# Three decoder-like blocks on one core: rotation by SBUF transfers, a later scaling, matmuls of a bank by kind

## The chip, the cores and the metric

The kernel runs on one core of a Trainium2 chip. The metric is device time in microseconds (us) from start to end of one execution; three executions of the kernel before gave 1177.98, 1178.29 and 1181.79 us, median 1178.29.

## The reference

A sequence of 256 rows of width 1024 in fp32 passes through one block of a first kind and two layers of a second kind. What touches the change is this:

```python
# first block, its end
x = x + jax.nn.sigmoid(x @ w_ple_gate[i]) * (p[i] @ w_ple[i])
return rms_norm(x, final_g)

# second block, per layer
h = rmsnorm(x, g_mix[l])
q_r, k_r, v_r, g_r, q_s, k_s, v_s, gate_a, gate_b = jnp.split(h @ w_in[l], splits, axis=-1)
q_r = rotary(q_r.reshape(B, S, RET_HEADS, RET_QK_DIM), pos)
k_r = rotary(k_r.reshape(B, S, RET_HEADS, RET_QK_DIM), pos) * (RET_QK_DIM ** -0.5)
...
x = x + merged @ w_out[l]
h = rmsnorm(x, g_mlp[l])
up = jnp.square(jax.nn.relu(h @ w_up[l]))
x = x + up @ w_down[l]

def rotary(t, pos):
    ...
    t1, t2 = t[..., :half], t[..., half:]
    return jnp.concatenate([t1 * cos - t2 * sin, t1 * sin + t2 * cos], axis=-1)
```

## The kernel before, in words

Activations stand transposed: 128 features on the partitions, the 256 rows of the sequence along the free axis, so that a tensor of width 1024 is 8 tiles of 128x256. All weights come as a stream of 189 chunks of 1 MB (128 x 2048 fp32). A chunk is fetched by SyncE (SP) into one of three `raw` buffers (`fetch`), then split into a rounded high part `wh` (ScalarE, line 286) and a remainder `wl` (VectorE, line 287), in two halves each (`split`). Activations are split in the same way (`hilo`, lines 127 and 128): a `Pair` holds high and low part of a tile beside each other, 512 columns in all. A product is then high x high, high x low and low x high, all on TensorE.

`mm_t` (line 289) multiplies a chunk of two 128-column blocks: for each block one PSUM bank `acc` (five of them), and for each of the 8 contraction tiles two matmuls. The first (line 295, called **h** here) has `wh` as the weights and streams 512 columns, the high and the low part of the activation at once, into the whole bank. The second (line 297, **l**) has `wl` as weights and streams the 256 columns of the high part into the first half of the bank. They alternate: h, l, h, l, 16 in a bank. `chunk_t` builds such a chunk; 136 of the 189 chunks are of this kind. `fold` (lines 313 and 314) then adds the two halves of the bank, ScalarE copying one and VectorE adding the other. `mm_n` (line 336) and `mm_2` (lines 131 to 133 by `mm3`) are two other forms: `mm_n` runs matmuls of 512 columns by kind, four of a kind in a row, and `mm_2` runs matmuls of 256 columns.

The loop at the end of `tile_blocks` (line 1007) issues per chunk: the split of chunk i+2, the fetch of chunk i+5, the matmuls and evictions of chunk i, and then one step of each waiting generator in `threads` (attention heads, `first_out` and others). The order written so is a starting point: the framework's scheduler reorders the instructions of each engine by a simulated timeline, within the data dependencies. Each engine and each DMA queue then runs its list strictly in order.

The rotation stands in `rot_evac` (lines 793 to 806), for 8 tiles per layer: after the fold, two VectorE products of 64 partitions each multiply the tile by sine and at the same time write the upper half of the partitions to the lower and the reverse (line 801); GpSimd multiplies by cosine (line 802) and adds (line 803); then `hilo`. The tables `n.cr` and `n.sr` (cosine and sine times the norm's factor) are made by `rotary_scales` on GpSimd once the norm's factor is there.

`first_out` (line 678) makes the first block's output, which is needed as residual: it computes the block's own norm factor and scales the 8 tiles of `X` on VectorE (line 687), one chunk after it is added to `threads`. `X` is next read when `w_out` of layer 0 is added to it, some 40 chunks on.

Of the kernel before, what the change touches and what calls it, by code (L numbers as in the profile page):

```python
# [21 lines left out]
S = 256  # L22
# [19 lines left out]
def _tables():  # L42
    f = np.float32
    c = np.zeros((P, C_ALL), f)
    i = np.arange(P)
    c[:, C_ID:C_ID + P] = np.eye(P)
    c[:, C_MQ:C_MQ + P] = np.where(i[None, :] > i[:, None], NEG, 0.0)
    c[:, C_MS:C_MS + P] = np.where(i[:, None] >= i[None, :], NEG, 0.0)
    c[:, C_TRI:C_TRI + P] = np.where(i[:, None] >= i[None, :], -1.0, 0.0)
    inv = (f(500000.0) ** (-np.arange(0, 16, 2, dtype=f) / f(16))).astype(f)  # L50
    ang = (np.arange(S, dtype=f)[:, None] * inv[None, :]).astype(f)
    co, si = np.cos(ang.astype(np.float64)).astype(f), np.sin(ang.astype(np.float64)).astype(f)
    for h in range(2):
        t = slice(h * P, (h + 1) * P)
        b = C_ROPE + 16 * h
        c[:, b:b + 8] = co[t]
        c[:, b + 8:b + 16] = co[t]
        b = C_ROPE + 32 + 16 * h
        c[:, b:b + 8] = -si[t]
        c[:, b + 8:b + 16] = si[t]  # L60
    inv = (f(10000.0) ** (-np.arange(64, dtype=f) / f(64))).astype(f)
    ang = (np.arange(S, dtype=f)[None, :] * inv[:, None]).astype(np.float64)
    c[:64, C_ROT:C_ROT + S] = np.cos(ang)
    c[64:, C_ROT:C_ROT + S] = np.cos(ang)
    c[:64, C_ROT + S:C_ROT + 2 * S] = np.sin(ang)
    c[64:, C_ROT + S:C_ROT + 2 * S] = -np.sin(ang)
    lg = np.log1p(-(2.0 ** (-5.0 - np.arange(4))))
    for h in range(4):
        b = C_DEC + 384 * h
        for off, q, k in ((0, 0, 0), (128, 128, 0), (256, 128, 128)):  # L70
            d = (q + i)[None, :] - (k + i)[:, None]
            c[:, b + off:b + off + P] = np.where(d >= 0, np.exp(lg[h] * np.maximum(d, 0)), 0.0) * 128 ** -0.5
    return c
# [3 lines left out]
def tile_blocks(ctx: ExitStack, tc: tile.TileContext, a: dict, out: bass.AP):  # L77
# [180 lines left out]
    class Chunk:  # L258
# [2 lines left out]


        def __init__(self, parts, banks, shape=(KT, S)):
            self.parts, self.banks, self.shape = parts, banks, shape

    def wcols(w, c, k0=0, kt=KT, n=S):
        return w, k0 * P, kt, c * n
# [20 lines left out]

    def mm_t(ch, ks, xs, j0, evac, n=2):

        for j in range(n):
            ps, w = acc(), slice((j0 + j) * P, (j0 + j + 1) * P)
            for i, (k, x) in enumerate(zip(ks, xs)):
                last = i == len(ks) - 1
                T.matmul(ps, lhsT=ch.wh[:, k, w], rhs=x.rearrange("p c t -> p (c t)"), start=i == 0, stop=last,  # L295
                         skip_group_check=True)
                T.matmul(ps[:, 0:S], lhsT=ch.wl[:, k, w], rhs=x[:, 0], start=False, stop=last, skip_group_check=True)  # L297
            run_pre()
            evac(ps, j)

# [9 lines left out]
    def fold(ps, out=None):  # L310

        t = tl([S], "f", bufs=NF) if out is None else out
        A.activation(t, ps[:, S:2 * S], AF.Copy)  # L313
        V.tensor_add(t, t, ps[:, 0:S])  # L314
        return t
# [27 lines left out]
            with tc.high_priority():  # L343
                pre.pop(0)()

    def chunk_t(w, c, x, evac, k0=0):
        def go(ch):
            mm_t(ch, range(KT), [x().t[:, k] for k in range(KT)], 0, lambda ps, j: evac(ps, 2 * c + j))
        chunks.append(Chunk([wcols(w, c, k0)], go))

    def chunk_2(w, c, x, evac, k0=0):
        def go(ch):
# [312 lines left out]
        hilo(st.n.x.h[:, k], st.n.x.l[:, k], X[:, k])  # L665

    for c in range(4):
        chunk_t(("w_out", 0), c, m_, out1_evac)

    def rotary_scales():  # L670
        n = st.n
# [6 lines left out]
    def first_out():  # L678

        n = st.n  # L680
        yield
        r = tl([W], "nv2")
        rsqrt(r, n.v1)
        yield
        r = r[:, 0:S]
        for k in range(KT):
            V.scalar_tensor_tensor(X[:, k], X[:, k], g_fin[:, k:k + 1], r, ALU.mult, ALU.mult)
            if k % 2:
                yield
# [87 lines left out]
    def layer(l):  # L777
# [15 lines left out]
        def rot_evac(w_):  # L793
            def f(ps, k):
                k -= 4 * w_
                if w_ == 0:
                    first(k)
                n = st.n
                t1, t2 = fold(ps), tl([S], "sig", bufs=4)
                for i, o in ((slice(64, 128), slice(0, 64)), (slice(0, 64), slice(64, 128))):  # L800
                    V.tensor_mul(t2[o], t1[i], n.sr[i])  # L801
                G.tensor_mul(t1, t1, n.cr)
                G.tensor_add(t1, t1, t2)
                d = sl(k // 2, w_)
                hilo(d[0][:, k % 2], d[1][:, k % 2], t1)
            return f

        for u in range(2):
            chunk_t(w, u, x_, rot_evac(0))
            chunk_t(w, 2 + u, x_, rot_evac(1))  # L810

            def ev(ps, h, u=u):
# [95 lines left out]
                yield  # L908

        for c in range(4):  # L910
            chunk_t(("w_out_2", l), c, m_, res_evac(g_mlp[l], mlp_in))

        ups = {}

# [10 lines left out]

        def up(g):
            for c in range(4):
                chunk_t(("w_up_2", l), 4 * g + c, x_, up_evac(g))

        def fin_add(c):  # L930
            def f(ps, h):
# [152 lines left out]
```

## Time and profile before

| what | value |
|---|---|
| median of 3 runs | 1178.29 us |
| the profiled execution | 1178.23 us |
| its span, first to last instruction | 1176.4 us |
| TensorE (PE) busy | 1161.2 us, 99% |
| weight loads of TensorE (PEld) busy | 1011.3 us, 86% |
| VectorE (DVE) busy | 886.9 us, 75% |
| ScalarE (ACT) busy | 706.7 us, 60% |
| GpSimd (POOL) busy | 230.4 us, 20% |
| mean granted TensorE clock | 0.996 |
| DMA | 204.47 MB, mean 174 GB/s |

The span leaves out 1.8 us around the instructions. A matmul's row shows when it starts and how long it takes until its end; the next begins before that end, so the price of a matmul in a stream is the distance of two starts, not its duration.

### The profile page before, as it was taken

What the parts mean: (1) busy time and instruction counts of PE and PEld (TensorE: products, weight loads), DVE (VectorE), ACT (ScalarE), POOL (GpSimd) and SP (SyncE); (2) the same over time, 40 slices, a digit from 0 to 9 for tenths busy, and PEclk for the clock granted to TensorE, in tenths of its full rate; (3) what the DMA queues carried; (4) which work ended last, traced back from release to release, by engine and by line L of the source; (5) the groups of instructions that cost most, each with busy time, mean ns of one, the idle gap of its engine ahead of it and who ended that gap; (6) DMA issues with size and microseconds to landing.
All of it is one profiled execution on the core that took longest, in us unless ns stands there. A gap on an engine that the chain in (4) does not pass through costs nothing.

```text
span 1176.4 us, 17442 instructions
## 1 busy us (share of the span) xinstructions
PE 1161.2 (99%) x6642; PEld 1011.3 (86%) x6642; DVE 886.9 (75%) x1449; ACT 706.7 (60%) x1275; POOL 230.4 (20%) x242
## 2 busy tenths in 40 slices
PE   8999999999999999999999999999999999999997
PEld 6888889997888888888888888888888888888887
DVE  6776768878989676568977777997776667867664
ACT  6657556566457776546745546556867565856452
POOL 1023104124462122202000002653112222000001
PEclk9999999999999999999999999999999999999999
DMA  8443434545335444545555555445444555555540
GB/s 309 180 143 144 146 114 160 202 180 203 144 143 179 148 163 155 190 169 185 209 191 203 180 185 217 162 161 182 159 145 157 190 191 192 184 182 199 192 179 36
DMA packets 29603, 204.47 MB, mean 174 GB/s; under 512 B 3408, under 2 KB 3664, under 8 KB 5584
## 3 DMA queue, kind: packets, MB, share of 16 engines
q1 hardware_dynamic: 29376, 203.34, 48.0%
q8 instruction: 52, 0.85, 0.3%
q14 instruction: 31, 0.25, 0.1%
q10 hardware_dynamic: 144, 0.03, 0.0%
HBM read 202.31 MB, written 1.05 MB: 173 GB/s over the span
## 4 chain that ended last, share of the span: by engine, by line
PE 93%; DVE 5%; issue 1%; ACT 0%; DMA 0%; POOL 0%; POOLq 0%; DVEq 0%; ACTq 0%
PE acc L295 41%; PE acc L297 21%; PE acc L336 19%; PE aux L131 2%; PE aux L133 2%; PE aux L132 1%; PE acc L131 1%; PE acc L132 1%; PE acc L133 1%; DVE wl L287 1%; DVE sig L801 1%; PE aux L458 1%; PE aux L764 1%; PE acc L324 1%; DMA X<-in_xt_dram 0%
## 5 line engine op out<-in xcount | busy, mean ns | idle before, releaser
L287 DVE TENSOR_TENSOR wl<-raw,wh 128x1024 fp32r<-128x1024 f32 (+1 forms) x380 | 463.2, 1253 | 154.4 <-ACT wh L286 152.2
L295 PE MATMUL acc<-X,wh 128*128 128x512 f32 x1472 | 524.7, 398 | 2.5 <-DVE vl L387 1.8
L286 ACT ACTIVATE wh<-raw 128x1024 fp32r<-128x1024 f32 (+1 forms) x380 | 380.7, 1047 | 200.2 <-PE acc L295 131.8
L297 PE MATMUL acc<-X,wl 128*128 128x256 f32 x1472 | 412.6, 281 | 0.0
L295 PEld LDWEIGHTS acc<-X,wh 128*128 128x128 f32 x1472 | 276.6, 188 | 64.5 <-DVE vl L387 2.1
L297 PEld LDWEIGHTS acc<-X,wl 128*128 128x128 f32 x1472 | 278.5, 189 | 2.3
L336 PE MATMUL acc<-wh,X 128*128 128x512 f32 x432 | 112.2, 392 | 0.0
L313 ACT ACTIVATE f<-acc 128x256 f32<-128x256 f32 x216 | 78.7, 372 | 42.2 <-PE acc L297 42.0
L314 DVE TENSOR_TENSOR f<-f,acc 128x256 f32<-128x256 f32 x216 | 86.4, 413 | 22.1 <-ACT f L313 21.3
L336 PEld LDWEIGHTS acc<-wh,X 128*128 128x128 f32 x432 | 79.7, 188 | 15.9
L295 PE MATMUL acc<-A,wh 128*128 128x512 f32 x256 | 90.2, 396 | 0.0
L295 PE MATMUL acc<-B,wh 128*128 128x512 f32 x256 | 90.1, 396 | 0.0
L207 POOL TENSOR_TENSOR sq<-sq,f 128x256 f32<-128x256 f32 x30 | 31.5, 1050 | 268.2 <-ACT f L205 267.6
L589 POOL TENSOR_TENSOR sig<-f,nr 128x256 f32<-128x256 f32 x48 | 42.5, 893 | 148.5 <-DVE f L314 148.4
L297 PE MATMUL acc<-B,wl 128*128 128x256 f32 x256 | 71.4, 279 | 0.0
L297 PE MATMUL acc<-A,wl 128*128 128x256 f32 x256 | 71.3, 279 | 0.0
L295 PE MATMUL acc<-M,wh 128*128 128x512 f32 x192 | 67.1, 397 | 0.0
L658 DVE TENSOR_TENSOR X<-X,acc 128x256 f32<-128x256 f32 x112 | 45.3, 416 | 24.8 <-PE acc L297 23.7
L336 PE MATMUL acc<-wl,X 128*128 128x512 f32 x216 | 59.5, 393 | 0.0
L295 PEld LDWEIGHTS acc<-B,wh 128*128 128x128 f32 x256 | 48.1, 188 | 11.6
L295 PEld LDWEIGHTS acc<-A,wh 128*128 128x128 f32 x256 | 48.1, 188 | 11.3
L297 PE MATMUL acc<-M,wl 128*128 128x256 f32 x192 | 52.7, 280 | 0.0
(224 smaller groups left out, 1744.6 us busy)
## 6 DMA issues: line engine op xcount, KB each, us to landing
raw<-in_wstream_dram SPq DMA_DIRECT2D x187, 1024.0 KB, 4.8
raw<-in_wstream_dram SPq DMA_DIRECT2D x4, 512.0 KB, 7.7
B<-in_tables_dram SPq DMA_DIRECT2D x2, 768.0 KB, 6.8
X<-in_xt_dram SPq DMA_DIRECT2D x2, 512.0 KB, 6.3
out_dram<-M SPq DMA_DIRECT2D x4, 256.0 KB, 2.2
M<-in_g_final_dram SPq DMA_DIRECT2D x1, 512.0 KB, 3.7
cst<-in_tables_dram SPq DMA_DIRECT2D x1, 352.0 KB, 10.0
B<-in_pt_dram SPq DMA_DIRECT2D x1, 256.0 KB, 2.7
```

Source lines behind the costliest of these rows:

```text
L131: T.matmul(o, lhsT=lh, rhs=rh, start=start, stop=False, skip_group_check=True)
L133: T.matmul(o, lhsT=ll, rhs=rh, start=False, stop=stop, skip_group_check=True)
L207: (V if k == KT - 1 else G).tensor_add(sq, sq, t)
L286: A.activation(ch.wh[:, k], ch.raw[:, k], AF.Copy)
L287: V.tensor_sub(ch.wl[:, k], ch.raw[:, k], f32(ch.wh[:, k]))
L295: T.matmul(ps, lhsT=ch.wh[:, k, w], rhs=x.rearrange("p c t -> p (c t)"), start=i == 0, stop=last, skip_group_check=True)
L297: T.matmul(ps[:, 0:S], lhsT=ch.wl[:, k, w], rhs=x[:, 0], start=False, stop=last, skip_group_check=True)
L313: A.activation(t, ps[:, S:2 * S], AF.Copy)
L314: V.tensor_add(t, t, ps[:, 0:S])
L336: T.matmul(p[:, 0:w], lhsT=xs[:, k, t], rhs=ws[:, i, o], start=n == 0 and k == 0, stop=n == 2 and k == KT - 1, skip_group_check=True)
L589: G.tensor_mul(store[(c, i)][0][:, k % 2], fold(ps), st.n.rb)
L658: V.tensor_add(X[:, k], X[:, k], ps[:, o:o + S])
```

## The change

Four edits:

- In `mm_t` the 16 matmuls of a bank are issued by kind, first the 8 h and then the 8 l, unless the chunk is marked `fresh`. Marked are the first chunk behind a norm or a merge: of `w_out`, of the rotated queries, of `w_out_2` and of `w_up_2`, 7 chunks in all.
- In `rot_evac` two transfers from SBUF to SBUF on SP's queue write the halves of the folded tile, exchanged, into the second half of a `sig` buffer; GpSimd writes the product with cosine into the first half; VectorE multiplies the exchanged tile by sine in one instruction of 128 partitions; GpSimd adds.
- The sign of the sine table is turned over, since it is now applied behind the exchange.
- `first_out` waits for twenty steps instead of one.

```diff
     def mm_t(ch, ks, xs, j0, evac, n=2):
         for j in range(n):
             ps, w = acc(), slice((j0 + j) * P, (j0 + j + 1) * P)
-            for i, (k, x) in enumerate(zip(ks, xs)):
-                last = i == len(ks) - 1
-                T.matmul(ps, lhsT=ch.wh[:, k, w], rhs=x.rearrange("p c t -> p (c t)"), start=i == 0, stop=last,
-                         skip_group_check=True)
-                T.matmul(ps[:, 0:S], lhsT=ch.wl[:, k, w], rhs=x[:, 0], start=False, stop=last, skip_group_check=True)
+            kinds = [[(i, n) for i in range(len(ks)) for n in range(2)]] if ch.fresh else \
+                [[(i, n) for i in range(len(ks))] for n in range(2)]
+            for i, n_ in sum(kinds, []):
+                k, x = ks[i], xs[i]
+                if n_ == 0:
+                    T.matmul(ps, lhsT=ch.wh[:, k, w], rhs=x.rearrange("p c t -> p (c t)"), start=i == 0, stop=False,
+                             skip_group_check=True)
+                else:
+                    T.matmul(ps[:, 0:S], lhsT=ch.wl[:, k, w], rhs=x[:, 0], start=False, stop=i == len(ks) - 1,
+                             skip_group_check=True)
             run_pre()
             evac(ps, j)
...
     def first_out():
         n = st.n
-        yield
+        for _ in range(20):
+            yield
         r = tl([W], "nv2")
         rsqrt(r, n.v1)
...
-                t1, t2 = fold(ps), tl([S], "sig", bufs=4)
+                t, s2 = fold(ps), tl([2, S], "sig", bufs=4)
+                t1, t2 = s2[:, 0], s2[:, 1]
                 for i, o in ((slice(64, 128), slice(0, 64)), (slice(0, 64), slice(64, 128))):
-                    V.tensor_mul(t2[o], t1[i], n.sr[i])
-                G.tensor_mul(t1, t1, n.cr)
+                    load(t2[o], t[i])
+                G.tensor_mul(t1, t, n.cr)
+                V.tensor_mul(t2, t2, n.sr)
                 G.tensor_add(t1, t1, t2)
```

How the built order moves is shown at three places. The line numbers of the changed kernel are 7 to 9 higher behind `mm_t`: h is line 300, l is 303, the fold's sum 321, the values' low part 395, the sine product 813.

TensorE, one bank of a gate chunk of layer 0 (`acc` is the bank, `wh` and `wl` the chunk's two parts, `X` the normed activation). Before, the beginning of the bank's 16 rows, of which 16 more follow for the second bank:

```order
L295 MATMUL acc_3423<-X_384_2489,wh_3319 128x512
L297 MATMUL acc_3423<-X_384_2489,wl_3320 128x256
L295 MATMUL acc_3423<-X_384_2489,wh_3319 128x512
L297 MATMUL acc_3423<-X_384_2489,wl_3320 128x256
L295 MATMUL acc_3423<-X_384_2489,wh_3319 128x512
L297 MATMUL acc_3423<-X_384_2489,wl_3320 128x256
```

Of the change, both banks of the same chunk and those of the next:

```order
L300 MATMUL acc_3392<-X_384_2489,wh_3312 128x512 x8
L303 MATMUL acc_3392<-X_384_2489,wl_3313 128x256 x8
L300 MATMUL acc_3416<-X_384_2489,wh_3312 128x512 x8
L303 MATMUL acc_3416<-X_384_2489,wl_3313 128x256 x8
```

The kinds stand apart. In the whole built order an h is directly followed by an l 365 times, where it was 2,100 times.

VectorE, the first four rotated tiles of layer 0 (`f` the folded tiles, `sig` the products with sine, `sr` the sine table, `nr` the norm's factor, `vl` the low part of the retention's values, whose bank it frees). Before:

```order
L233 SCALAR_TENSOR_TENSOR nr_2776<-nt_2792,nr_2776 128x260
L287 TENSOR_TENSOR wl_2993<-raw_2853,wh_2992 128x1024 x2
L801 TENSOR_TENSOR sig_2813<-f_2810,sr_2800 64x256 x2
L801 TENSOR_TENSOR sig_2840<-f_2837,sr_2800 64x256 x2
L801 TENSOR_TENSOR sig_2875<-f_2872,sr_2800 64x256 x2
L801 TENSOR_TENSOR sig_2902<-f_2899,sr_2800 64x256 x2
L387 SCALAR_TENSOR_TENSOR vl_2973<-acc_2924,nr_2776,vh_2972 128x512
```

Of the change:

```order
L321 TENSOR_TENSOR f_2902<-f_2902,acc_2885 128x256
L287 TENSOR_TENSOR wl_2948<-raw_2745,wh_2947 128x1024 x2
L231 TENSOR_TENSOR nt_2792<-nr_2776,nv_426_2778 128x260
L232 SCALAR_TENSOR_TENSOR nt_2792<-nt_2792,nr_2776 128x260
L233 SCALAR_TENSOR_TENSOR nr_2776<-nt_2792,nr_2776 128x260
L287 TENSOR_TENSOR wl_2986<-raw_2855,wh_2985 128x1024
L813 TENSOR_TENSOR sig_2813<-sig_2813,sr_2800 128x256
L813 TENSOR_TENSOR sig_2841<-sig_2841,sr_2800 128x256
L813 TENSOR_TENSOR sig_2877<-sig_2877,sr_2800 128x256
L813 TENSOR_TENSOR sig_2905<-sig_2905,sr_2800 128x256
L395 SCALAR_TENSOR_TENSOR vl_2968<-acc_2921,nr_2776,vh_2967 128x512
```

Four products stand where eight stood, one half of a split has moved behind `vl`, and between the last fold (`f_2902`) and the product that needs its exchange (`sig_2905`) stand three halves of splits, three rows of the norm and three products.

SP's queue at the same place (`raw` are the weight chunks, `B` a table). Before:

```order
L124 DMA B_437_2808<-in_tables_dram 128x1536
L124 DMA raw_2853<-in_wstream_dram 128x2048
L124 DMA raw_2922<-in_wstream_dram 128x2048
L124 DMA raw_2958<-in_wstream_dram 128x2048
L124 DMA raw_2998<-in_wstream_dram 128x2048
```

Of the change:

```order
L124 DMA B_437_2808<-in_tables_dram 128x1536
L124 DMA sig_2813<-f_2810 64x256 x2
L124 DMA raw_2855<-in_wstream_dram 128x2048
L124 DMA sig_2841<-f_2838 64x256 x2
L124 DMA sig_2877<-f_2874 64x256 x2
L124 DMA raw_2919<-in_wstream_dram 128x2048
L124 DMA sig_2905<-f_2902 64x256 x2
L124 DMA raw_2953<-in_wstream_dram 128x2048
```

The exchanges, two per tile and 32 in all, stand among the fetches in the same queue, each behind its fold; the fetches behind them wait in the queue with them.

## Rows read from the trace of the kernel before

**Rows 1.** The page: the chain that ended last, shares of the span by engine.
```profile
PE 93%; DVE 5%; issue 1%; ACT 0%; DMA 0%; POOL 0%; POOLq 0%; DVEq 0%; ACTq 0%
```

**Rows 2.** Waits of PE: engine, line, waited for, total us, times, longest.
```profile
PE acc L295 <- DVE vl L387: 1.8, 1, 1.8
PE aux L133 <- DVE pl L128: 1.5, 2, 1.1
PE acc L295 <- DVE f L314: 0.7, 1, 0.7
```

**Rows 3.** Windows, the whole span, line 297 alone: PE, PEld, clock, DMA.
```profile
0.00:1176.00 1176.00, 608.10 (x2176) 411.03 (x2176) 1.00 0.48 174
```

**Rows 4.** Timeline of PE: start, us, engine, line, tiles; two stretches that alternate.
```profile
452.32 0.40 PE L295 MATMUL acc<-A,wh 128*128 128x512 f32 x1
...
518.39 0.40 PE L295 MATMUL acc<-M,wh 128*128 128x512 f32 x1
...
550.94 0.40 PE L295 MATMUL acc<-X,wh 128*128 128x512 f32 x1
...
719.08 0.39 PE L295 MATMUL acc<-X,wh 128*128 128x512 f32 x1
```

**Rows 5.** Timeline of PE: 512 columns behind 512 columns (line 336, by kind).
```profile
1126.82 1.07 PE L336 MATMUL acc<-wl,A 128*128 128x512 f32 x4
...
1130.45 0.39 PE L336 MATMUL acc<-wh,A 128*128 128x512 f32 x1
```

**Rows 6.** Timeline of PE: 256 columns behind 256 columns (lines 131 to 133).
```profile
235.94 0.28 PE L131 MATMUL acc<-A,wh 128*128 128x256 f32 x1
...
240.74 0.28 PE L132 MATMUL acc<-A,wh 128*128 128x256 f32 x1
```

**Rows 7.** Timeline of PE: four pairs in which kinds stand together by chance.
```profile
524.39 0.62 PE L295 MATMUL acc<-M,wh 128*128 128x512 f32 x2
...
525.80 0.40 PE L295 MATMUL acc<-M,wh 128*128 128x512 f32 x1
```

**Rows 8.** Timeline of PE around its longest wait [idle before, releaser].
```profile
290.89 0.28 PE L297 MATMUL acc<-X,wl 128*128 128x256 f32 x1
292.97 0.61 PE L295 MATMUL acc<-X,wh 128*128 128x512 f32 x1 [1.80 <-DVE vl L387]
...
296.72 0.39 PE L295 MATMUL acc<-X,wh 128*128 128x512 f32 x1
```

**Rows 9.** Timeline of DVE in the same place.
```profile
286.77 5.36 DVE L801 TENSOR_TENSOR sig<-f,sr 64x256 f32<-64x256 f32 x8
292.17 1.41 DVE L387 SCALAR_TENSOR_TENSOR vl<-acc,nr,vh 128x512 fp32r<-128x512 f32 x2
```

**Rows 10.** Lines of DVE, 282 to 346 us: busy us, mean ns | idle before.
```profile
L287 DVE TENSOR_TENSOR wl<-raw,wh 128x1024 fp32r<-128x1024 f32 x18 | 24.7, 1403 | 0.8 <-ACT wh L286 0.7
L801 DVE TENSOR_TENSOR sig<-f,sr 64x256 f32<-64x256 f32 x16 | 10.9, 680 | 0.4
L314 DVE TENSOR_TENSOR f<-f,acc 128x256 f32<-128x256 f32 x10 | 3.9, 407 | 1.4 <-ACT f L313 1.4
...
L687 DVE SCALAR_TENSOR_TENSOR X<-X,gc,nv 128x256 f32<-128x256 f32 x8 | 3.3, 473 | 0.0
```

**Rows 11.** Windows: stretch, PE, PEld, DVE, ACT, POOL busy, granted clock, DMA, GB/s.
```profile
282.00:302.00 20.00, 18.20 (x95) 15.51 (x94) 19.01 (x26) 12.41 (x20) 15.36 (x15) 0.91 0.48 181
390.00:420.00 30.00, 30.00 (x170) 26.20 (x170) 20.48 (x33) 21.83 (x43) 3.91 (x5) 1.00 0.47 169
```

**Rows 12.** Timeline of POOL: the sine table.
```profile
283.90 1.76 POOL L675 TENSOR_TENSOR sr<-cst,nr 128x256 f32<-128x256 f32 x1
```

**Rows 13.** Line 124, all transfers of SP: time from issue to landing.
```profile
DMA to landing us min/median/max: 2.1/4.8/10.8
```

**Rows 14.** Timeline of PE: one h and the l behind it in the slower rhythm.
```profile
222.87 0.40 PE L295 MATMUL acc<-M,wh 128*128 128x512 f32 x1
223.11 0.28 PE L297 MATMUL acc<-M,wl 128*128 128x256 f32 x1
```

More of the change, by code (lines that the diff above doesn't have):

```diff
@@ L64, in _tables @@
     c[64:, C_ROT:C_ROT + S] = np.cos(ang)
-    c[:64, C_ROT + S:C_ROT + 2 * S] = np.sin(ang)
-    c[64:, C_ROT + S:C_ROT + 2 * S] = -np.sin(ang)
+    c[:64, C_ROT + S:C_ROT + 2 * S] = -np.sin(ang)
+    c[64:, C_ROT + S:C_ROT + 2 * S] = np.sin(ang)
     lg = np.log1p(-(2.0 ** (-5.0 - np.arange(4))))
@@ L263, in __init__ @@
         def __init__(self, parts, banks, shape=(KT, S)):
-            self.parts, self.banks, self.shape = parts, banks, shape
+            self.parts, self.banks, self.shape, self.fresh = parts, banks, shape, False
     def wcols(w, c, k0=0, kt=KT, n=S):
@@ L344, in run_pre, with chunk_t @@
                 pre.pop(0)()
-    def chunk_t(w, c, x, evac, k0=0):
+    def chunk_t(w, c, x, evac, k0=0, fresh=False):
         def go(ch):
@@ L349, in chunk_t @@
         chunks.append(Chunk([wcols(w, c, k0)], go))
+        chunks[-1].fresh = fresh
     def chunk_2(w, c, x, evac, k0=0):
@@ L667, in tile_blocks @@
     for c in range(4):
-        chunk_t(("w_out", 0), c, m_, out1_evac)
+        chunk_t(("w_out", 0), c, m_, out1_evac, fresh=c == 0)
     def rotary_scales():
@@ L808, in layer @@
         for u in range(2):
-            chunk_t(w, u, x_, rot_evac(0))
+            chunk_t(w, u, x_, rot_evac(0), fresh=u == 0)
             chunk_t(w, 2 + u, x_, rot_evac(1))
@@ L910, in layer @@
         for c in range(4):
-            chunk_t(("w_out_2", l), c, m_, res_evac(g_mlp[l], mlp_in))
+            chunk_t(("w_out_2", l), c, m_, res_evac(g_mlp[l], mlp_in), fresh=c == 0)
         ups = {}
@@ L927, in up @@
             for c in range(4):
-                chunk_t(("w_up_2", l), 4 * g + c, x_, up_evac(g))
+                chunk_t(("w_up_2", l), 4 * g + c, x_, up_evac(g), fresh=g == 0 and c == 0)
         def fin_add(c):
```

## The prediction

> **What bounds the kernel now.** I read the page first. TensorE makes 93% of the chain that ended last [rows 1], and the table above has it busy for 99% of the span: the time is what PE needs for its list, plus the moments in which it waits. So a change can shorten the run in two ways: a lower price per matmul, or fewer waits of PE. Then the waits of PE: behind the start-up only a few are left, and the four that count all name VectorE as the releaser, 4.0 us together [rows 2]. Then the timeline, for the price of a matmul, which is the distance from one start to the next.
>
> The alternating matmuls run in one of two rhythms. From 452.32 to 518.39 us 187 pairs of h and l follow one another, 353.3 ns a pair; from 550.94 to 719.08 us 485 pairs, 346.7 ns a pair [rows 4]. The reader is to see that the two stretches do the same work at full clock. I counted all stretches of over twenty pairs with nothing between: 1,708 pairs, of which 1,170 are within 0.001 us of the slow rhythm and 538 of the fast one; the mean is 350.7 ns. There are 2,176 pairs in all [rows 3]. What puts a stretch into one rhythm or the other the trace does not say.
>
> The same sizes by kind are in the trace too, in the other two forms. 512 columns behind 512 columns: 16 matmuls from 1126.82 to 1130.45 us, 226.9 ns each [rows 5]. 256 behind 256: 40 matmuls from 235.94 to 240.74 us, 120.0 ns each [rows 6]. Together 346.9 ns, which is the fast rhythm.
>
> **The change part by part.**
>
> *Matmuls by kind.* No matmul and no weight load is added or taken away. In the built order an h directly in front of an l stands 365 times where it stood 2,100 times, so 1,735 pairs leave the alternation. At the mean of 350.7 and a by-kind price of 346.7 (the fast rhythm; rows 5 and 6 agree with it within their rounding) each gives 4.0 ns back: 1,735 x 4.0 = **6.9 us**. The bounds: at most all 2,176 pairs, 8.7 us; at least nothing, since at a place where the scheduler had put kinds together by chance four pairs took 1.41 us, 352.5 ns each [rows 7], the slow rhythm. Below nothing: by kind could settle at the slow rhythm throughout, 1,735 x (353.3 - 350.7) = 4.5 us lost, or worse (rival C). I take 6.9, because rows 5 and 6 are long runs and rows 7 is four pairs that begin and end in alternation. A bank's last high-part matmul now comes half a bank earlier in need of the second half of `wh`; splits are made two chunks ahead, some 11 us (32 pairs), which hides half a microsecond; without that cover PE would wait up to 0.5 us a bank for ScalarE. `wl` is needed later than before.
>
> *VectorE's rotation.* In layer 0 eight tiles cost sixteen products, 10.9 us between 282 and 346 us, mean 680 ns [rows 10]. Eight products of 128 partitions take their place: 407 ns each if nothing disturbs them (the sum of the fold, same shape [rows 10]), up to 680 ns if GpSimd's products beside them slow them as the present ones are; 3.3 to 5.4 us. VectorE gets 5.5 to 7.6 us back there.
>
> *The later scaling.* Eight rows of line 687, 3.3 us [rows 10], and the norm factor's three small ones leave the same stretch, where VectorE is busy 19.01 of 20 us at its start [rows 11]. They come back some twenty chunks on, about 400 us, where VectorE is busy 20.48 of 30 us [rows 11]: they cost nothing there; without that cover they would cost their 3.3 us. ACT's two functions go with them, and its table loads are 13 in both orders.
>
> *What that does to PE.* Its longest wait begins behind the matmul at 290.89 us: the next bank is free only when the values' low part has been read from it, and that stands behind the eight half products of 286.77 us [rows 8, 9]. PE goes on at 292.97 us, 1.97 us late by starts. And then the granted clock is lower: the window from 282 to 302 us shows 0.91 of full speed [rows 11], and six pairs from 292.97 to 296.72 us take 3.75 us where they take 2.10 at 0.350 each [rows 8]: the lower of the two levels, 1.2 GHz, for most of these microseconds behind an idle of two, worth 1.65 us. In the changed order the four products may begin when the sine table is there, 285.66 us [rows 12]; at 407 ns [rows 10] to 670 ns each (5.36/8 [rows 9]) they end by 288.4, and the first half of the values 0.7 us on, at 289.1, before 290.9. So the wait and the clock's fall go. The other waits stand behind the same backlog: VectorE is ahead by over 5 us then, and they are at most 1.1 us each [rows 2]. Sum of what can go: 4.0 us of waits, 0.7 for the overlap that each of the four loses besides, 0.17 in the longest (1.97 by starts against 1.80), 1.65 of clock: 6.4. I take **5.6 us** and leave 0.8 to waits that only shift; bounds 6.4 and 0.
>
> *The transfers.* 32 of 64 KB each are added. The trace has none from SBUF to SBUF; the nearest rows are SP's transfers, 2.1 us at the least, 4.8 in the middle, 10.8 at most from issue to landing [rows 13]. I take 2.2 to 4.8, since the smallest large ones are four times this size. Covers: between the fourth tile's fold and its product VectorE has three halves of splits (1.4 each [rows 10]) and three products (0.41), 5.4 us without the norm's small rows; in the second group of four one half of a split and eight other instructions of at least 0.41, 4.7 us. Up to that a landing costs nothing. The Trainium skill, "DMA: Bandwidth & Descriptors", section "Anatomy of one DMA", puts a fixed 2.0 us and the bytes at 436 GB/s on a transfer from GpSimd's queue, 2.15 us here as an estimate; no run so far shows one from SBUF to SBUF. On SP's queue each stands in front of a fetch and may hold it until a fold is there, a chunk at most (16 pairs, 5.6 us); a fetch is issued three chunks (17 us) ahead of its split and lands in 4.8, so 12 us are spare. I cost it at nothing; if that cover were short, it would be `wh` that is late next.
>
> GpSimd has as many instructions as before, and its product no longer waits for VectorE's reading. Evictions keep their number.
>
> **Sum**, against the profiled execution of 1178.23 us, which is the median of the three runs (1178.29): 1178.2 - 6.9 - 5.6 = **1165.7 us**.
>
> **The rivals.**
>
> *Order is indifferent (A).* The pair costs what it costs, as the four pairs of rows 7 say, and only VectorE's relief counts: 1178.2 - 5.6 = 1172.6. Against it stand the long runs of rows 5 and 6. The Trainium skill, "TensorE: Matmul & The Clock Gate", section "Back-to-back issue gap", speaks for it: its gap, N/2.4 + 2.5 ns warm, depends on the columns alone, 215.8 + 109.2 = 325 ns a pair in either order. By it the term would be 0 and the time 1172.6. The trace disagrees with the figure (346.7 to 353.3) and shows two prices for one sum of columns [rows 4]. Chance 0.17.
>
> *VectorE's relief does not arrive (B).* The products wait for landings as long as they used to compute, so PE's waits stay: 1178.2 - 6.9 = 1171.3. For it: 4.8 us in the middle is near the covers of 4.7 and 5.4, and a fetch of 1 MB may be in flight in front of the exchange. Against it: the size, and the smallest rows at 2.1. If every landing took the worst row's 10.8 us, VectorE would stand 5.4 us in the first group and 6.1 in the second, 11.5 a layer, against some 10 it gets back in layer 0 and 6.5 in layer 1, where no scaling is moved: PE would lose 6.5 us more, 1177.8, which I leave outside the range. Chance 0.12.
>
> *A rhythm of its own (C), the side of slower.* In a run by kind every h would cost what an h costs in the slow rhythm at its worst, 240 ns [rows 14], and every l behind an l 120 [rows 6]: 360 ns a pair in place of 350.7. Over 1,735 pairs that is 16.1 us: 1178.2 + 16.1 - 5.6 = 1188.7. The result is slower from about 356 ns a pair on, where the loss passes 5.6 + 3.5 us. For it: that two rhythms exist shows that a stream can lock to more than one step. Against it: rows 5 hold the same size at 226.9 over a long run, and rows 6 the same operands. Chance 0.04.
>
> *Neither part does anything (D):* kinds indifferent and the waits kept, 1178.2. Chance 0.04.
>
> **How the numbers follow.** Forecast 0.63, A 0.17, B 0.12, C 0.04, D 0.04. The likeliest is 1165.7; its own range, with 6.9 between 4 and 8.7 and 5.6 between 4 and 6.4, is 1163.1 to 1170.2. A and B lie above it, at 1171.3 and 1172.6, and with half of the other's term lost reach 1174.5; below that only an eviction that starts earlier, the first half of a bank being complete 0.96 us before its end, could give more. Range **1162 to 1174.5**. What a measurement of this kernel can tell from no change is about 0.3%, 3.5 us: faster means under 1174.8. Nearly all of the forecast, A and B lie there, so faster 0.88, same 0.07 (D and the edge of A and B), slower 0.05 (C and the edge of D).
>
> **What would show it.** By kind: in any gate or MLP chunk 512-column starts 227 ns apart, then 256-column starts 120 ns apart, 2.78 us a bank; 2.81 to 2.83 says A. VectorE: no wait of PE on line 395 near 291 us and granted clock 1.00 from 282 to 302; products of line 813 of 0.4 to 0.7 us without idle in front of them. An idle of VectorE that names a transfer in front of line 813 says B. Eight rows of line 696 near 400 us with PE without idle there. An h behind an h at 236 ns or more says C. Wrong in size it would be if the two rhythms were there by kind as well, or if PE's waits came back with another name, ScalarE's or SP's.

## The result and the profile after

The changed kernel takes 1169.14 us, median of 4 runs (1168.73 to 1170.5), against 1178.55 before, median of 4 (1177.98 to 1181.79). The ratio is 0.9915, with a 95% interval of 0.9899 to 0.993: faster by 9.4 us, where 12.5 were forecast. The time lies in the range given, 3.4 us above the number. The profiled execution took 1168.73 us, its span 1167.0.

Line numbers have moved: h is now line 300 (295 before), l line 303 (297), the fold 320 and 321 (313, 314), the values' low part 395 (387), the scaling 696 (687), the untransposed matmul 343 (336), and the rotation's products 812 and 813.

The page of the changed kernel, its line of PE and the chain by engine [rows 1]:

```profile
PE 1155.9 (99%) x6642; PEld 1013.0 (87%) x6642; DVE 876.3 (75%) x1433; ACT 707.4 (61%) x1275; POOL 221.2 (19%) x242
...
PE 94%; DVE 4%; ACT 1%; issue 1%; DMA 0%; POOLq 0%; POOL 0%; DVEq 0%
```

PE was the bound and still is, so the gain is in how its list runs. The waits of PE after [rows 2]; the first two are the start-up's:

```profile
PE acc L331 <- ACT wh L286: 2.2, 1, 2.2
PE aux L416 <- DVE one_r L152: 1.3, 1, 1.3
PE acc L343 <- DVE f L321: 0.5, 1, 0.5
PE acc L300 <- DVE X L666: 0.4, 2, 0.2
PE acc L300 <- DVE f L321: 0.2, 1, 0.2
```

All four waits that the prediction counted are gone. The last three rows, 1.1 us together, are new: the kernels below that have by kind bank by bank with the evictions where the change has them (e2, e4, e5, e11) show the same three, and those that alternate throughout (before, e1, e8, e10) show none of them. The windows of [rows 11], after:

```profile
282.00:302.00 20.00, 19.99 (x122) 17.71 (x121) 18.93 (x24) 12.20 (x22) 17.50 (x17) 1.00 0.50 185
390.00:420.00 30.00, 30.00 (x174) 26.55 (x173) 25.14 (x42) 21.65 (x41) 6.05 (x5) 1.00 0.47 166
```

In the first stretch PE runs through, 122 matmuls instead of 95, and the granted clock is 1.00 where it was 0.91. In the second VectorE has 25.14 us to do instead of 20.48, and PE is still busy for the whole 30: the scaling costs nothing where it now stands. The timelines of DVE, then of POOL, where the old half products were [rows 9]:

```profile
282.58 1.29 DVE L287 TENSOR_TENSOR wl<-raw,wh 128x1024 fp32r<-128x1024 f32 x1 [1.81 <-ACT wh L286]
283.79 3.61 DVE L813 TENSOR_TENSOR sig<-sig,sr 128x256 f32<-128x256 f32 x4
287.32 1.40 DVE L395 SCALAR_TENSOR_TENSOR vl<-acc,nr,vh 128x512 fp32r<-128x512 f32 x2
```
```profile
281.55 0.75 POOL L683 TENSOR_TENSOR sr<-cst,nr 128x256 f32<-128x256 f32 x1
282.39 0.86 POOL L684 TENSOR_SCALAR rbs<-nr 128x256 f32<-128x256 f32 x1
283.33 3.79 POOL L812 TENSOR_TENSOR sig<-f,cr 128x256 f32<-128x256 f32 x4
```

Four products end by 287.4 and the values' low part by 288.7; before, this part only began at 292.17. Nothing idles between them.

Now the matmuls by kind. The timeline of PE in the layer-0 MLP, then in a place that is entered from the 512-column matmuls of line 343:

```profile
599.80 1.12 PE L303 MATMUL acc<-X,wl 128*128 128x256 f32 x8
600.75 2.00 PE L300 MATMUL acc<-X,wh 128*128 128x512 f32 x8
602.59 1.11 PE L303 MATMUL acc<-X,wl 128*128 128x256 f32 x8
603.54 2.00 PE L300 MATMUL acc<-X,wh 128*128 128x512 f32 x8
605.38 1.11 PE L303 MATMUL acc<-X,wl 128*128 128x256 f32 x8
606.34 2.00 PE L300 MATMUL acc<-X,wh 128*128 128x512 f32 x8
```
```profile
731.58 1.07 PE L343 MATMUL acc<-wh,X 128*128 128x512 f32 x4
732.49 1.98 PE L300 MATMUL acc<-X,wh 128*128 128x512 f32 x8
734.30 1.11 PE L303 MATMUL acc<-X,wl 128*128 128x256 f32 x8
735.25 2.00 PE L300 MATMUL acc<-X,wh 128*128 128x512 f32 x8
737.10 1.11 PE L303 MATMUL acc<-X,wl 128*128 128x256 f32 x8
```

Eight h behind l take 1.84 us (600.75 to 602.59), eight h behind 512-column matmuls 1.81 (732.49 to 734.30). From the starts of 166 banks entered from l: the h steps are 233, 236, 228, 232, 231 ns and only then 227, the l steps 113, 119 and then 120; a bank takes 2.793 us, with next to no spread (80% of them between 2.793 and 2.794), in all parts of the program. Entered from line 343 (9 banks) every h step is 226 to 228 ns on average and the bank takes 2.766 us in the median. So by kind has one price, 349.1 ns a pair (2.793/8): better than the slow alternating rhythm (353.3), worse than the fast one (346.7) [rows 4], and the layer-0 MLP, which alternated in the fast one, now runs slower than before.

Where the 9.5 us came from, by the starts of PE's matmuls (first to last start 1168.65 us before, 1159.19 after). I split the 6,641 steps by how far each lies above its floor, the columns at 2.4 GHz plus 13.3 ns, which is what [rows 5] and [rows 6] show:

| steps above the floor by | before | after | difference |
|---|---|---|---|
| over 150 ns (waits, 512 columns at the lower clock) | 15.97 us | 10.76 | -5.2 |
| 20 to 150 ns (changes of shape, small waits, 256 columns at the lower clock) | 28.08 | 26.63 | -1.5 |
| up to 20 ns (rhythm, entries) | 7.24 | 4.44 | -2.8 |

The forecast had 6.9 in the last row and 5.6 above it. By stretches, the first two rows together fell by 5.7 us between 278 and 346 us (7.4 to 1.8) and by 0.7 between 720 and 790 (2.2 to 1.5), where the rotated tiles are made. They fell by 1.1 between 140 and 180 us, where a wait of 0.7 us on ScalarE went that no part of the working aimed at, and rose by 0.8 in the rest of the program.

### The profile page after: what moved, and what is told of

It reads as the page before. It is cut to its first block, busy times and chain, and to the rows that moved or that the text cites. A ratio compares the mean times of both kernels' runs of the same rounds, so it can differ in the third digit from the quotient of the medians.

```text
span 1167.0 us, 17530 instructions
## 1 busy us (share of the span) xinstructions
PE 1155.9 (99%) x6642; PEld 1013.0 (87%) x6642; DVE 876.3 (75%) x1433; ACT 707.4 (61%) x1275; POOL 221.2 (19%) x242
## 4 chain that ended last, share of the span: by engine, by line
PE 94%; DVE 4%; ACT 1%; issue 1%; DMA 0%; POOLq 0%; POOL 0%; DVEq 0%
PE acc L300 41%; PE acc L303 21%; PE acc L343 20%; DVE wl L287 2%; PE aux L131 2%; PE aux L133 2%; PE aux L132 2%; PE acc L133 1%; PE acc L132 1%; PE acc L131 1%; DVE X L666 1%; PE aux L466 1%; PE aux L773 1%; DVE X L197 1%; PE acc L331 1%
## 5 line engine op out<-in xcount | busy, mean ns | idle before, releaser
L300 PE MATMUL acc<-X,wh 128*128 128x512 f32 x1472 | 383.1, 394 | 0.6 <-DVE X L666 0.4
L300 PEld LDWEIGHTS acc<-X,wh 128*128 128x128 f32 x1472 | 263.5, 189 | 47.9 <-issue 1.2
L303 PE MATMUL acc<-X,wl 128*128 128x256 f32 x1472 | 221.5, 283 | 0.0
L303 PEld LDWEIGHTS acc<-X,wl 128*128 128x128 f32 x1472 | 206.8, 190 | 13.6
L300 PE MATMUL acc<-A,wh 128*128 128x512 f32 x256 | 64.5, 393 | 0.0
L300 PE MATMUL acc<-B,wh 128*128 128x512 f32 x256 | 64.4, 392 | 0.0
L300 PE MATMUL acc<-M,wh 128*128 128x512 f32 x192 | 53.0, 394 | 0.0
L343 PEld LDWEIGHTS acc<-wl,X 128*128 128x128 f32 x216 | 40.0, 188 | 7.8
L300 PEld LDWEIGHTS acc<-M,wh 128*128 128x128 f32 x192 | 35.0, 188 | 6.9
L303 PEld LDWEIGHTS acc<-A,wl 128*128 128x128 f32 x256 | 35.1, 190 | 2.5
```

The lines of the kernel that those rows point to most:

```text
L343: T.matmul(p[:, 0:w], lhsT=xs[:, k, t], rhs=ws[:, i, o], start=n == 0 and k == 0, stop=n == 2 and k == KT - 1, skip_group_check=True)
```

## The experiments

**Theories.** *Forecast*: by kind is worth 6.9 us. *Entry*: a run of 512 columns behind a run of 256 pays some 27 ns over its first five matmuls, of which the l run gives 7 to 8 back; by kind is worth about 3. *Rival A*: order is worth nothing. For VectorE: does either relief do, or are both needed?

**e1, the order undone.**

```diff
-            kinds = [[(i, n) for i in range(len(ks)) for n in range(2)]] if ch.fresh else \
-                [[(i, n) for i in range(len(ks))] for n in range(2)]
+            kinds = [[(i, n) for i in range(len(ks)) for n in range(2)]]
```

> The change with all its chunks in the alternating order (h, l, h, l), the new rotation and the later scaling kept. Forecast's term (by kind is worth 6.9 us): 1169.1 + 6.9 = 1176.0 us. Entry theory (in the trace of the change a 512-column matmul follows another at 227 ns only from the sixth on; the first five behind a run of 256-column ones take 233, 236, 228, 232 and 231, so a bank takes 2.793 us everywhere, between the two alternating rhythms of 2.774 and 2.826): by kind is worth about 3 us, 1172.1 us, and alternating banks show both rhythms again. Rival A (order is indifferent): 1169.1 us. By every theory the four waits of PE on VectorE near 286 to 297 us stay away here if the rotation and the scaling removed them; if they come back, by kind had removed them.

Measured: 1171.41 us (1168.54 to 1173.31), ratio 0.9928 [0.9914, 0.9943]. So by kind is worth 2.3 us by medians (3.7 by the starts in the two profiled executions), not 6.9. Its share in the small steps is 6.42 - 4.44 = 2.0 us, and that is the part to rely on. By the time alone it is not clear of the noise: the interval of this ratio overlaps that of the change, and e1's executions run from 1168.54 us at a mean granted clock of 0.999 to 1173.31 at 0.993, those of the change from 0.996 to 0.997. In e1's profiled execution the clock fell in a place where it did not in the change; the window, e1 and then the change:

```profile
157.00:166.00 9.00, 8.85 (x41) 8.06 (x42) 6.59 (x20) 6.73 (x18) 0.00 (x0) 0.62 0.01 2
```
```profile
157.00:166.00 9.00, 8.95 (x63) 8.14 (x63) 7.27 (x23) 7.09 (x17) 0.00 (x0) 1.00 0.08 28
```

Between 140 and 180 us the steps more than 20 ns above the floor take 8.2 us in e1 and 4.8 in the change (5.9 in the kernel before), more than the whole of what the 3.7 hold beside the small steps. Whether the order has to do with that fall no run shows. The waits near 286 to 297 us stay away, so the two VectorE parts removed them. The timeline of PE in this kernel shows the chance in the rhythms:

```profile
451.96 0.40 PE L299 MATMUL acc<-B,wh 128*128 128x512 f32 x1
...
513.32 0.39 PE L299 MATMUL acc<-M,wh 128*128 128x512 f32 x1
```

177 pairs in 61.36 us are 346.7 ns a pair: the stretch that ran slow before, at 353.3 [rows 4], ran fast here, though its order is the same.

**e2, the order alone**, in the kernel before (the diff is the change's parts in `mm_t`, `Chunk` and `chunk_t`, with its marks for the chunks that alternate).

> The kernel before with by kind alone (old rotation, scaling at once). Forecast's term: 1178.5 - 6.9 = 1171.6 us. Entry theory: 1178.5 - 3 = 1175.5 us. Both keep PE's waits on VectorE near 286 to 297 us, of about 4 us; a PE that arrives there a little sooner may wait up to 0.5 us longer.

Measured: 1179.17 us, ratio 0.9999 [0.9989, 1.0009]: nothing. Both theories missed. The small steps fell as they did in the change, 7.24 to 4.47 us, so the price per matmul was saved; but the waits and slow steps over 150 ns rose from 15.97 to 20.41. The waits of PE in e2, and its window:

```profile
PE acc L300 <- DVE vl L395: 2.4, 1, 2.4
PE aux L131 <- ACT M L127: 2.2, 2, 1.7
PE acc L331 <- ACT wh L286: 1.7, 1, 1.7
PE aux L416 <- DVE one_r L152: 1.3, 1, 1.3
PE aux L133 <- DVE M L128: 1.0, 1, 1.0
```
```profile
282.00:302.00 20.00, 15.39 (x72) 12.86 (x71) 19.72 (x31) 9.76 (x14) 12.84 (x12) 0.83 0.24 96
```

VectorE is busy 19.72 of 20 us: it sets the pace there, the matmuls saved upstream arrive early and wait, and the granted clock falls to 0.83 behind those waits. By stretches, the steps more than 20 ns above the floor rose by 1.3 us between 278 and 346 us and by 1.3 between 720 and 790, where the rotated tiles are made. Another 1.0 us each came before 140 us and between 346 and 720, which this account does not cover.

**e3, by kind over both banks of a chunk.**

```diff
-        for j in range(n):
-            ps, w = acc(), slice((j0 + j) * P, (j0 + j + 1) * P)
+        pss, m = [acc() for _ in range(n)], range(len(ks))
...
+            order = [[(j, i, 0) for j in range(n) for i in m] + [(0, i, 1) for i in m]] + \
+                [[(j, i, 1) for i in m] for j in range(1, n)]
```

> The change with by kind carried over both banks of a chunk: sixteen 512-column matmuls into two banks, then sixteen 256-column ones. Entry theory (a price of about 27 ns each time a run of 512 columns follows a run of 256): some 130 of 254 entries go, 130 x 27 ns = 3.5 us, so 1165.6 us; 512-column steps are 227 ns in the second bank of a chunk. If the price follows the length of the run of 256 columns ahead (sixteen rather than eight), the entry doubles to about 54 ns and the time stays at 1169.1 us. Rival: the two evictions of a chunk now come 1 us apart rather than 2.8, and PE waits for banks or for VectorE: above 1170 us with such waits in the list.

Measured: 1177.94 us, ratio 0.9991 [0.9982, 1.0], almost the whole gain lost. The entry part came as expected: a chunk behind l takes 5.567 us in 55 of 55 places, and all small steps together 2.27 us (4.44 in the change); the entry does not grow with the length of the l run ahead. What it cost stands in the waits of PE:

```profile
PE acc L302 <- DVE X L197: 3.4, 2, 1.9
PE acc L345 <- DVE f L323: 2.3, 1, 2.3
```

The two evictions of a chunk now come about 1 us apart, and ahead of a norm (line 197) and of the untransposed chunks (345) PE waits for VectorE to finish them. Behind the two longest of these waits the granted clock fell as well, where the change has 1.00; the windows of e3:

```profile
85.00:100.00 15.00, 12.67 (x59) 10.29 (x59) 9.09 (x19) 14.07 (x37) 10.90 (x14) 0.89 0.04 7
535.00:550.00 15.00, 13.15 (x60) 10.54 (x59) 9.12 (x17) 4.65 (x12) 3.07 (x3) 0.89 0.40 142
```

**e4, the scaling at once** (the first diff), **e5, the old rotation** (the second), each in the change; **e8**, the later scaling alone, and **e10**, the new rotation alone, each in the kernel before.

```diff
-        for _ in range(20):
-            yield
+        yield
```
```diff
-                for i, o in ((slice(64, 128), slice(0, 64)), (slice(0, 64), slice(64, 128))):
-                    load(t2[o], t[i])
-                G.tensor_mul(t1, t, n.cr)
-                V.tensor_mul(t2, t2, n.sr)
+                for i, o in ((slice(64, 128), slice(0, 64)), (slice(0, 64), slice(64, 128))):
+                    V.tensor_mul(t2[o], t1[i], n.sr[i])
+                G.tensor_mul(t1, t1, n.cr)
```

> The change with block 1's output scaled at once (one step of its thread, not twenty). If the rotation alone relieved VectorE: 1169.1 us, no wait of PE on VectorE near 286 to 297 us. If the later scaling did: four waits of about 4 us in all and a lower granted clock at 282 to 302 us come back, 1173 to 1175 us. The forecast's own working (products of 0.4 us rather than 1.4 leave about 3.9 us of VectorE's surplus, the later scaling takes about 11 us of work out of that stretch) gives most of it to either one alone, so 1169 to 1171 us.

> The change with the old rotation (two VectorE half products of 1.4 us that cross the partitions, no transfers), the later scaling and by kind kept. e4 showed the later scaling worth 6.6 us beside the other two. If VectorE is relieved once and either part could have done it (the forecast's working), the rotation adds little on top: 1169 to 1170.5 us and no wait of PE on VectorE over 1 us near 286 to 297 us. If both parts are needed there (twenty steps later the scaling still falls on a VectorE that is behind by its half products): waits of 2 to 4 us come back, 1172 to 1174 us. If the transfers themselves cost something that was overlooked, it is faster than the change: below 1169 us.

> The kernel before with the later scaling alone (old rotation, all banks alternating). If the scaling alone relieves VectorE: 1178.5 - 5.6 (the forecast's whole relief) to 7 = 1171.5 to 1173 us, no wait of PE on VectorE over 1 us near 286 to 297 us. If both parts are needed: 1175 to 1178 us with such waits left.

> The kernel before with the new rotation alone (scaling at once, all banks alternating). The runs so far say that each of the two reliefs of VectorE is worth 5 to 6.6 us beside the other two parts, and that the scaling alone gave 3.5 us. If the two reliefs add up (both together gave 7.0 us): 1178.3 - 3.5 = 1174.8 us. If the rotation works only with the scaling out of the way: 1177 to 1178.5 us, with the waits near 286 to 297 us left. If the transfers cost by themselves: above 1178.5 us.

With e1 and e2 these give all eight combinations, each against the kernel before on the same chip:

| rotation | scaling | by kind | ratio, 95% | median us |
|---|---|---|---|---|
| old | at once | no | 1 | 1178.5 |
| old | at once | yes (e2) | 0.9999 [0.9989, 1.0009] | 1179.17 |
| old | later | no (e8) | 0.9968 [0.9956, 0.998] | 1174.82 |
| new | at once | no (e10) | 0.9971 [0.9959, 0.9984] | 1175.62 |
| new | later | no (e1) | 0.9928 [0.9914, 0.9943] | 1171.41 |
| new | at once | yes (e4) | 0.9966 [0.9954, 0.9978] | 1175.72 |
| old | later | yes (e5) | 0.9958 [0.9945, 0.997] | 1174.41 |
| new | later | yes (the change) | 0.9915 [0.9899, 0.993] | 1169.14 |

Each relief alone gives about 3 to 3.5 us, both together 7: they add, and my expectation that either would do for the other was wrong. They act on different waits: e8 keeps the wait of 1.8 us on the values' low part and a clock of 0.91 from 282 to 302 us, e10 loses it but waits 2.4 us for a fold (line 314).

By the medians, by kind gives nothing while either relief is missing (+0.7, -0.4, +0.1 us) and 2.3 us with both. Each of these differences is uncertain by some 1 to 2 us, by the intervals of the two ratios that it stands between, so only the first, e2, is more than a hint: 2.8 us were saved in the small steps and did not reach the end. The steps say more. By kind takes 2.8 us from the small ones with neither relief, 1.5 (e5 against e8) and 2.7 (e4 against e10) with one, and 2.0 with both. To those more than 20 ns above the floor, in the two stretches of the rotated tiles (278 to 346 and 720 to 790 us), it adds 2.7 us with neither, 0.1 and 1.3 with one, and 0.4 with both. The window from 278 to 345 us shows where PE is held up; first the kernel before, then e10, e4, e5, e1 and the change:

```profile
278.00:345.00 67.00, 63.25 (x345) 54.18 (x344) 63.55 (x99) 35.01 (x60) 36.16 (x33) 0.97 0.45 169
```
```profile
278.00:345.00 67.00, 64.50 (x357) 55.69 (x356) 62.25 (x95) 36.59 (x63) 36.10 (x36) 0.97 0.55 193
```
```profile
278.00:345.00 67.00, 63.52 (x350) 55.10 (x349) 59.77 (x94) 36.73 (x63) 37.90 (x35) 0.97 0.53 186
```
```profile
278.00:345.00 67.00, 65.04 (x366) 56.07 (x365) 60.87 (x100) 36.85 (x63) 41.21 (x39) 1.00 0.48 171
```
```profile
278.00:345.00 67.00, 66.97 (x380) 58.04 (x379) 60.32 (x102) 38.92 (x66) 37.86 (x39) 1.00 0.58 199
```
```profile
278.00:345.00 67.00, 66.99 (x388) 58.71 (x387) 61.40 (x103) 39.65 (x69) 41.59 (x42) 1.00 0.54 188
```

PE's busy time is the first number behind the 67.00, then its matmuls. Only with both reliefs is PE busy for the whole stretch. e5 keeps a granted clock of 1.00 here and still loses 2 us to waits, and 1.5 more where layer 1 does the same: from 740 to 785 us, e5 and then the change:

```profile
740.00:785.00 45.00, 43.44 (x249) 37.74 (x248) 42.20 (x66) 23.33 (x40) 23.18 (x23) 1.00 0.39 140
```
```profile
740.00:785.00 45.00, 44.97 (x265) 39.70 (x264) 40.95 (x65) 25.30 (x45) 22.82 (x23) 1.00 0.57 199
```

No scaling is moved in layer 1, so there the rotation has to do it alone.

**e6, half runs.**

```diff
-                [[(i, n) for i in range(len(ks))] for n in range(2)]
+                [[(i, n) for i in q] for q in pairs(range(len(ks))) for n in range(2)]
```

> The change with its runs of a kind cut in halves (4 h, 4 l, 4 h, 4 l of a bank). Entry theory, price per entry of a 512-column run: the first four 512-column steps behind 256-column ones carry 22.9 ns over 227, the first 256-column step gives 6.6 ns back, so 16 ns more a bank; by some 250 banks 4.1 us: 1173.2 us and banks of 2.81 us. If the price hangs on the length of the 256-column run ahead (four rather than eight), it stays at 1169.1 us; if short runs fall into the fast alternating rhythm, 2.774 us a bank, 1164.5 us.

Measured: 1171.82 us (1170.38 to 1174.08), ratio 0.9938 [0.9924, 0.9953]. A half bank takes 1.403 us on average in some 400 places, 2.806 a bank, 13 ns more than the change's 2.793; the small steps together are 6.98 us, 2.5 more. By medians 2.7 us were lost, of 4.1 expected: more entries cost time, with a smaller price each than I had reckoned.

**e7, both banks only inside**, as e3 where another transposed chunk that does not alternate follows:

```diff
+    for c_, d_ in zip(chunks, chunks[1:]):
+        c_.both = c_.t and not c_.fresh and d_.t and not d_.fresh
```

> As e3 (by kind over both banks of a chunk), but only in chunks that another transposed chunk with all its input ready follows; those ahead of a norm, of the untransposed chunks or of a chunk that alternates go bank by bank as in the change. In e3 a joined chunk took 5.567 us rather than 2 x 2.793 = 5.586 (19 ns less), and PE's waits of 3.4 us at the two MLP norms, 2.3 us ahead of an untransposed chunk and the lower clock behind them cost 9 us. Entry theory: some 80 to 100 joined chunks x 19 ns = 1.5 to 1.9 us, so 1167.4 us, with none of e3's waits. If closer evictions as such hurt, not their place ahead of a norm: 1170 us or more.

Measured: 1174.26 us, ratio 0.996 [0.9947, 0.9972]. The expectation failed: the small steps fell to 2.73 us, but waits at the norms (1.8 us) and at line 345 (0.8) stayed (3.4 and 2.3 in e3). To leave the last chunk alone is not enough to be rid of them, and which of the chunks before it makes VectorE late there I did not single out. They are not all of the loss: of the 4.9 us by which e7's profiled execution is longer than the change's, by the starts, 3.7 lie between 140 and 180 us, where the clock fell as in e1:

```profile
157.00:166.00 9.00, 9.00 (x42) 8.39 (x43) 6.43 (x21) 5.72 (x16) 0.00 (x0) 0.62 0.00 0
```

**e9, the second bank mirrored**: h then l in bank 0, l then h in bank 1, evictions 2.8 us apart as in the change.

```diff
-                [[(i, n) for i in range(len(ks))] for n in range(2)]
-            for i, n_ in sum(kinds, []):
+                [[(i, n) for i in range(len(ks))] for n in ((0, 1), (1, 0))[j % 2]]
+            order = sum(kinds, [])
+            for q, (i, n_) in enumerate(order):
```

(`start` and `stop` go to the first and last matmul of `order`.)

> The change with the second bank of each by-kind chunk mirrored: bank 0 takes its 512-column matmuls and then its 256-column ones, bank 1 its 256-column ones first and then its 512-column ones. So a run of 512 columns is entered once in two banks, as in e3, but the evictions stay 2.8 us apart. Entry theory: 19 ns less a chunk, as e3's 5.567 against 5.586 us, by some 110 to 125 by-kind chunks 2.1 to 2.4 us, plus nothing lost on VectorE: 1167.0 us, two banks in 5.567 us. If it was not the eviction's place but the order over two banks that cost e3 and e7 their waits: 1172 us or more, with waits at the MLP norms again.

Measured: 1167.42 us (1167.04 to 1169.21), ratio 0.9904 [0.9889, 0.992], as the entry theory had it. The timeline of PE:

```profile
601.28 3.82 PE L301 MATMUL acc<-X,wh 128*128 128x512 f32 x16
604.93 2.08 PE L304 MATMUL acc<-X,wl 128*128 128x256 f32 x16
606.84 3.82 PE L301 MATMUL acc<-X,wh 128*128 128x512 f32 x16
```

Sixteen h and sixteen l in 5.56 us (601.28 to 606.84); a bank whose h follow h takes 2.766 us (some 80 places), as one entered from line 343. No wait at the norms: the order of matmuls over two banks does not cost anything by itself. What is left for e3 is the place of the evictions, or that it takes two banks at once; its waits name the evictions, and no run tells the two apart.

**e11 and e12, side by side on one chip**: the change again, and the mirror with alternation kept in the first bank only of the chunks behind a norm or merge (`if ch.fresh and j == 0`).

> The change itself once more, on the chip of the next kernel, so that the two can be held against each other: 1169.1 us. Its by-kind banks behind a run of 256 columns take 2.793 us again if the entry is a property of the order; another value if it is a chance of the run.

> As e9 (mirrored second banks), and the chunks behind a norm or merge alternate in their first bank only: by the end of that bank all their inputs are ready, so the second needs no alternation. Entry theory: e9's 1167.4 us less some 7 banks x 40 ns at most (2.826 to 2.79) = 0.3 us: 1167.2 us, and 1.5 to 2.5 us below the change on the same chip. If e9's gain over the change was a difference between chips: level with the change.

Measured: 1169.32 us (1169.03 to 1169.68) for the change and 1167.54 (1167.28 to 1168.81) for e12, ratios 0.9913 [0.9898, 0.9928] and 0.9901 [0.9885, 0.9917]. The intervals of the ratios overlap, but no run of the one falls among the runs of the other: 1.8 us, about what the entries were worth (small steps 4.44 and 2.17 us). The by-kind bank of 2.793 us came back in all of 166 places. e12's own addition to e9 cannot be told from nothing. The mirrored kernel is the fastest of the study.

## Why the prediction was right or wrong

**By kind, 6.9 us: right in kind, too large.** The step that failed is "1,735 x 4.0", and in it the by-kind price of 346.7 ns. It was added up from two long runs, [rows 5] and [rows 6], each of which stands in its own kind; the place where one kind takes over from the other was costed at nothing, though a bank has it twice. It measured 349.1 ns, so (350.7 - 349.1) x 1,735 = 2.8 us, which is what the small steps show. Beside it the new order brought the 1.1 us of waits shown above, which the working had at nothing. [Rows 7], which I set aside because the four pairs began and ended in alternation, already held such changes of kind in short runs and showed 352.5. The prediction's count of pairs is off, without effect on the sum: the stretches of over twenty pairs hold about 1,380 pairs, some 840 of them slow and 538 fast, and their mean is 350.7 as stated.

**By kind, whose gain it is.** The sum treated the two terms as independent. They are not: by kind alone gave nothing (e2), in good part because PE came earlier to a VectorE that was late anyway. Rival B's 1171.3 is thereby wrong too: by e2, had the relief not arrived, by kind would have been worth nothing either.

**PE's waits on VectorE, 5.6 us: right, a little small.** The longest wait, the clock's fall behind it and the waits behind the same backlog went, as the working had it. e1, which has these parts alone, is 7.1 us faster by medians. Of its steps more than 20 ns above the floor 6.0 us went between 278 and 346 us and 0.7 between 720 and 790; 6.4 was put down as all that can go. The price of a product was set too low at its upper end: 0.4 to 0.68 us, and line 813 took

```profile
L813 DVE TENSOR_TENSOR sig<-sig,sr 128x256 f32<-128x256 f32 x8 | 5.8, 748 | 0.1
```

over layer 0's eight, 0.9 us for each of the first four. VectorE's own saving there was 10.9 - 5.8 = 5.1 us where 5.5 to 7.6 were taken, without effect on the end.

**The transfers, nothing: right.** The page of the changed kernel and the one wait on them (line 813):

```profile
sig<-f SPq DMA_DIRECT2D x32, 64.0 KB, 4.6
```
```profile
  DMA sig<-f: 0.5, 1
```

The median of 4.6 us is near the upper end that I took, 4.8, although each is a sixteenth of a weight fetch. The one wait cost VectorE 0.5 us. A split on ScalarE waited once for a weight fetch, 1.0 us, as none did before. No wait of PE names a transfer. The estimate of 2.15 us that the prediction set beside it from the Trainium skill, "DMA: Bandwidth & Descriptors", section "Anatomy of one DMA", was for another queue; on this queue, with the weights' fetches on it too, the trace shows twice that.

**The later scaling, nothing at its new place: right.** Eight rows from 398.1 to 400.8 us, and PE busy throughout.

**The rivals.** A (order indifferent, 1172.6) is nearer in the time than in the mechanism: a bank takes neither 2.78 nor 2.81 to 2.83 us. The formula that the prediction sets beside A from the Trainium skill, "TensorE: Matmul & The Clock Gate", section "Back-to-back issue gap", is given there for a matmul that stands alone; for this stream the 346.7 to 353.3 ns of the trace decide. Of C, the rhythm of its own, there is a trace: an h behind an h does take 236 ns, but once in a run. D fell.

**The range, in part luck.** The time lies within the forecast's own range, 1163.1 to 1170.2, but neither term lies within its own: by kind gave 2.8 where 4 was the least, and the steps above it 6.7 where 6.4 was the most. The two misses made up for each other in part. The upper end of the whole range does not follow from its reasons: with half of its term lost B reaches 1174.7 and A 1175.4, not 1174.5.

## What to carry to other kernels

Price a new order of instructions at its joints, not only in its long runs: read what the first few instructions behind a change of kind cost, and count the changes. A cheaper instruction on the engine that bounds can be worth nothing while the engine that feeds it is late, as in e2; relieve that one first, then look again. And before two profiled executions are compared, hold their granted clocks against each other stretch by stretch: e1 and the change differ by a fall of the clock whose cause no run shows. And where runs must alternate, mirror every second one: this halves the joints and leaves the evictions where they were.

## What the runs showed of the hardware

- The first five 512-column matmuls behind a run of 256-column ones take 233, 236, 228, 232 and 231 ns from start to start, and the later ones 227; behind 512-column ones 226 to 228 at once. The length of the run ahead matters little: behind 8 (the change) and behind 16 (e3) the first four steps are the same within 0.3 ns, behind 4 (e6) they are 234, 234, 232 and 229 on average. The matmuls' and weight loads' records do not say what is being made up.
- h and l in strict alternation lock to 346.7 or 353.3 ns a pair and can keep that for over 170 pairs; the same stretch took one in one program and the other in another. By kind, the time was the same to a few ns a bank in every kernel that had it.
- The multiplications of VectorE and GpSimd slow each other. The five rows of line 813 with no instruction of GpSimd beside them take 410 to 426 ns; the ten with one or two of GpSimd's multiplications beside them for over 0.6 us take 889 to 994. The timeline of DVE has both in a row, GpSimd idle beside the first:

```profile
311.97 0.41 DVE L813 TENSOR_TENSOR sig<-sig,sr 128x256 f32<-128x256 f32 x1
312.31 0.40 DVE L321 TENSOR_TENSOR f<-f,acc 128x256 f32<-128x256 f32 x1
312.64 0.89 DVE L813 TENSOR_TENSOR sig<-sig,sr 128x256 f32<-128x256 f32 x1
```

GpSimd's line 812 takes 737 to 745 ns beside line 744 of VectorE, which reads one tile, and 915 to 1140 beside line 813. The Trainium skill, "SBUF — State Buffer", section "SBUF: two separate sides", gives one pair of ports to a VectorE operation with two SBUF inputs and to GpSimd, held in turn for a whole instruction; the rows agree with such turns.
